# Engine order of the feed-forward products from a list of operations with durations and due times, and all low halves of the weights made on VectorE

## The chip, the cores and the metric

One core of a Trainium2 chip. A core has TensorE (PE, matrix products), VectorE (DVE), ScalarE (ACT), GpSimd (POOL) and the SP queue, each with an instruction queue of its own that runs in order and waits on semaphores; 16 DMA engines move data. The metric is the time of one execution on the device in microseconds, lower is better. "Row" below is a row of the profile or of an engine's instruction order.

## The reference

One block of a hybrid network on 256 tokens of 2048 channels, in float32: a feed-forward, a mixer (an RWKV recurrence and a pooling branch, gated), and a second feed-forward, each with a norm ahead and behind.

```python
def _swiglu(x, w_gate, w_up, w_down):          # w_gate, w_up: 2048 x 5632, w_down: 5632 x 2048
    return (jax.nn.silu(x @ w_gate) * (x @ w_up)) @ w_down

f = _swiglu(_rmsnorm(h, ln_ffn1_pre), ffn1_gate, ffn1_up, ffn1_down)
h = h + 0.5 * _rmsnorm(f, ln_ffn1_post)
mx = _hybrid_mixer(_rmsnorm(h, ln_mix_pre), w_in, ..., w_out)
h = h + _rmsnorm(mx, ln_mix_post)
f = _swiglu(_rmsnorm(h, ln_ffn2_pre), ffn2_gate, ffn2_up, ffn2_down)
h = h + 0.5 * _rmsnorm(f, ln_ffn2_post)
```

## The kernel before

**Numbers in halves.** Each weight tile `w` (128 x 1024, two rows of 128 x 512) is loaded by SP's queue, ScalarE casts it to a rounded high half `wH`, and VectorE subtracts to get the low half `wL`. A product is three matmuls of 128 x 512 (`mm3`, lines 178 to 180: high by high, high by low, low by high), once for each half `h` of the 256 tokens. Four buffers hold loaded tiles (`W32_BUFS`), five hold `wH` and `wL` (`WS_BUFS`).

**Blocks.** A feed-forward computes gate and up in 11 blocks of 512 columns. Blocks 0 and 1 are plain products. Blocks 2 to 10 (`FAST`, function `seven`) take gate (`wf`, banks f0 and f1) and up (`wl`, banks l0 and l1) together: three *quads* each replace eight products by seven through sums of the weights (`t13`, `t24`, made by VectorE in lines 407, 411 and 415; both are shown as `t`) and sums of the input (`sm`, function `sums`), into extra banks shown as `ms`; the other ten *pairs* are plain, twelve matmuls each. When the last quad is done, ScalarE copies one extra bank (line 446) and VectorE adds the others and then f0, f1, l0 and l1 (lines 449 and 465, all into tiles `u`), which empties those banks for the next block. After that come SiLU (line 750), the product of gate and up (line 754), VectorE's transposes into `T` (line 653) and 16 small transfers on GpSimd's queue (line 665, `x<-T`); ScalarE and VectorE split what arrived into halves again (`carry_at`, lines 677 and 681), the hidden rows for the down product. The down products (`post`, tables `DOWN`, `OUT`) use the same `seven` with 7 and 8 quads.

**What sets the order.** In the feed-forwards and in the last product of each stage the order on TensorE, ScalarE and VectorE is written by a recording layer: `put(t, fn)` appends matmuls with a length `t` and `at(t, fn)` gives other work a moment on that clock; `run` emits both by time. The moment of a tile's load and of both its halves is one and the same, when the slot of `WS_BUFS` comes free (`slot`). GpSimd's and SP's instructions are emitted in the same pass, and each of these two queues runs in the order of emission. The rest of the mixer is ordered by a scheduler.

**Blocks 3 to 6** (`PROBE`) treat one of their ten pairs (the up pair at row tile 12) differently, by `low_by` (line 325): it has a load of its own and halves outside the five slots, given in `seven` by `other`. ScalarE makes `dH` (line 335). The low half `dL` is made without VectorE: in the first feed-forward ScalarE writes the rounded `w` with its sign turned (line 337) and a transfer on GpSimd's queue adds `w` to it (line 341); in the second GpSimd subtracts (line 343). The three steps are emitted at fixed moments ahead of the product:

```python
        s.at(t - 24, get)
        s.at(t - 18, high)
        s.at(t - 17.9, low)
```

Of the kernel before, what the change touches and what calls it, by code (L numbers as in the profile page):

```python
# [14 lines left out]
ALU = mybir.AluOpType  # L15
# [23 lines left out]
TT = 0.45  # L39
NUNITS = 33  # L40
STAG = 10
TRAIL = 16
AHEAD = (5.0, 6.0)
TURNS = [[4.2, 5.3, 6.4, 7.5], [5.3, 6.0, 6.7, 7.4]]
WARM = 12
TB = 4
DOWN = ((0, 7, ((8, 12), (0, 3, 5, 7, 9)), 0),
        (2, 8, ((2, 4, 6, 8, 10, 12), (0, 2)), TRAIL))
OUT = ((0, 0, (), 0), (1, 2, ((4,), (0,)), 0), (3, 0, (), TRAIL))
FAST = range(2, 11)  # L50
PROBE = range(3, 7)
CARRY = (18, 21)
NG, SPOTS = 3, ((2, 4), (1,))
# [3 lines left out]
ROWS2 = [("r_k", 8), ("gn_w", 8), ("gn_b", 8), ("pool_scale", 8)]  # L57


class Block:  # L60
    def __init__(s, tc, ctx):
# [5 lines left out]
        s.late, s.after, s.items, s.events, s.now = [], [], deque(), [], 0.0  # L67
        s.clk, s.uses = 0.0, []
# [35 lines left out]
    def at(s, t, fn):  # L104

        s.n += 1
        heapq.heappush(s.events, (t, s.n, fn))

    def slot(s, end):

        s.uses.append(end)
        n = len(s.uses) - 1 - WS_BUFS
        return s.uses[n] if n >= 0 else n - 1.0

    def run(s):

        s.now = 0.0
        E = mybir.EngineType
        with s.tc.manual_schedule(engines={E.PE, E.Activation, E.DVE}):
            while s.items or s.events:  # L120
# [7 lines left out]
        s.now = s.clk = 0.0  # L128
        s.uses = []

    def put(s, t, fn):
        s.items.append((t, fn))
        s.clk += t
# [48 lines left out]
    def gemm_tok(s, w, c0, at, KT, evac, lead=False, trail=False, xs=None, hold=False,  # L182
                 order=None):
# [11 lines left out]
        def both(k0, k1):  # L195
            for k2 in order or range(k0, k1, 4):
                keep(s.load_w(w, k2, min(4, k1 - k2), c0, 512))
                for k in range(k2, min(k2 + 4, k1)):
                    do(k, 0)
                    do(k, 1)  # L200

        if trail:
            both(0, KT - TRAIL)
            s.by_half(w, c0, KT - TRAIL, KT, s.clk, AHEAD[0], do, keep,
                      lambda h: evac(h, pss[h]))
            return
        k0 = 0
        if xs:
            s.head(w, c0, KT, do, keep, xs)
            k0 = KT  # L210
        elif lead:
            s.by_half(w, c0, 0, STAG, s.clk, AHEAD[1], do, keep)
            s.run()
            k0 = STAG
        both(k0, KT)
        if hold:
            for h in range(2):
                s.at(0.3 + 1.6 * h, lambda h=h: evac(h, pss[h]))
            return
        with s.tc.high_priority(offset=BOOST):  # L220
            for h in range(2):
                evac(h, pss[h])

    def gemm_at(s, w, c0, at, KT, evac):

        pss = []
        ws = {}

        def load(k):
            ws.update((i, (wH, wL)) for i, wH, wL in s.load_w(w, k, 2, c0, 512))  # L230

        def do(k):
            if not pss:
                pss.extend(s.pm.tile([P, 512], F32, tag="mm", name=s.nm("mm"))
                           for _ in range(2))
            for h in range(2):
                (wH, wL), (xH, xL) = ws[k], at(k)
                s.mm3(pss[h], xH[:, h * P:h * P + P], xL[:, h * P:h * P + P], wH, wL,
                      k == 0, k == KT - 1)
        for k in range(0, KT, 2):  # L240
            s.at(s.slot(s.clk + 12 * MM), lambda k=k: load(k))
            s.put(6 * MM, lambda k=k: do(k))
            s.put(6 * MM, lambda k=k: do(k + 1))
        for h in range(2):
            s.at(s.clk + 0.3 + 1.6 * h, lambda h=h: evac(h, pss[h]))

    def by_half(s, w, c0, k0, k1, start, ahead, do, keep, done=None):

        for k in range(k0, k1, 2):
            s.at(start + (k - k0) * 3 * MM - ahead,  # L250
                 lambda k=k: keep(s.load_w(w, k, 2, c0, 512, k - k0 >= STAG)))
        for h in range(2):
            for k in range(k0, k1):
                s.put(3 * MM, lambda k=k, h=h: do(k, h))
            if done:
                s.put(0, lambda h=h: done(h))

    def sums(s, T, out, when, own=None, nq=2):
# [4 lines left out]
        fl = lambda t: t.rearrange("p a b t -> p (a b t)")  # L263

        def first():
            xH, xL = [t[:, :2 * nq].bitcast(F32).rearrange("p k t -> p (k t)")
                      for t in T[len(out) // 2]]
            x = tt["x"] = s.unit((P, 2, 2, S), F32, "sx")[:, :nq]
            V.tensor_tensor(out=fl(x), in0=xH, in1=xL, op=ALU.add)

        def second():
            x = tt["x"]
# [10 lines left out]
        def parts():  # L283

            j = len(out) // 2
            for n_ in ("sH", "sL"):
                if j % 2 == 0:
                    own["12" + n_] = s.unit((P, 2, 2, 2, P), F32R, n_)
                if j == 0:
                    own["4" + n_] = s.unit((P, 4, 2, P), F32R, n_)  # L290
            x = T[j]
            s3 = [u.rearrange("p (i b) t -> p i b t", b=2)[:, :, 0, P:] for u in x]
# [3 lines left out]
                       ([u[:, j] for u in s4], f[:, 3]), (s3, f[:, 2])]  # L296
# [3 lines left out]
        def lows():  # L300
# [3 lines left out]
            for i in range(2):  # L304
                out.append([(s12[0][:, m, i], s12[1][:, m, i]) for m in range(2)]
                           + [tuple(u[:, i] for u in v) for v in (s3, s4)])
# [9 lines left out]
        def fourth():  # L316
            f, fH, fL = tt["f"], tt["H"], tt["L"]
            V.tensor_tensor(out=fl(fL), in0=fl(f), in1=fl(fH).bitcast(F32), op=ALU.subtract)
            for i in range(nq):
                out.append([(fH[:, m, i], fL[:, m, i]) for m in range(4)])  # L320
        for i, fn in enumerate((first, second) + ((parts, lows) if own is not None
                                                  else (third, fourth))):
            s.at(when + 1.7 * i, fn)

    def low_by(s, how, w, k, c0, t, keep):

        nc = s.nc
        x = {}

        def get():  # L330
            x["w"] = s.get_w(w, k, 2, c0, 512, own=True)

        def high():
            x["H"], x["L"] = s.unit(dt=F32R, p="dH"), s.unit(dt=F32R, p="dL")
            nc.scalar.copy(x["H"], x["w"])
            if how == "dma":
                nc.scalar.activation(out=x["L"], in_=x["w"], func=AF.Copy, scale=-1.0)

        def low():
            if how == "dma":  # L340
                nc.gpsimd.dma_start(out=x["L"], in_=x["w"], accum_op=ALU.add)
            else:
                nc.gpsimd.tensor_tensor(out=x["L"], in0=x["w"], in1=x["H"].bitcast(F32),
                                        op=ALU.subtract)
            H, L = [x[n].rearrange("p (k c) -> p k c", k=2) for n in "HL"]
            keep([(k + i, H[:, i], L[:, i]) for i in range(2)])
        s.at(t - 24, get)
        s.at(t - 18, high)
        s.at(t - 17.9, low)

    def seven(s, wf, cf, wl, cl, at, KT, T, sm, n, spots, ev_first, ev_last, trail=0,
              one_end=False, ends=(-0.05, 2.7), other=None):
# [3 lines left out]
        V = nc.vector  # L356
        K0 = 2 * n

        bank = {}
        std = KT - K0  # L360
        left = dict(f0=std + n, f1=std, l0=std + n, l1=std + n, p1=n, p5=n, p6=n, p7=n)

        def mul(b, x, wt):
            left[b] -= 1
            new = b not in bank
            if new:
                bank[b] = s.psum("ms") if b[0] == "p" else s.pm.tile(
                    [P, 512], F32, tag="mm", name=s.nm("mm"))
            s.mm3(bank[b], *x, *wt, new, left[b] == 0)
# [4 lines left out]
        ws = {}  # L374

        def keep(tiles):
            ws.update((k, (wH, wL)) for k, wH, wL in tiles)

        def pair(k, w, c0, b):
            if other and (b, k) == other[1]:  # L380
                s.low_by(other[0], w, k, c0, s.clk, keep)
            else:
                s.at(s.slot(s.clk + 12 * MM), lambda: keep(s.load_w(w, k, 2, c0, 512)))
# [5 lines left out]
            s.put(12 * MM, do)  # L389
# [1246 lines left out]
```

## Time and profile before

| | |
|---|---|
| three executions, median (lowest to highest) | 2050.68 us (2049.8 to 2051.21) |
| profiled execution, first to last instruction (span) | 2047.8 us |
| TensorE, VectorE, ScalarE, GpSimd busy | 2019.4, 1741.7, 1161.5, 337.8 us |
| products of 128 x 512 into the plain banks (lines 178, 179, 180) | 3 x 2200 |
| TensorE's granted clock, mean | 0.997 of full speed |
| transfers | 425.66 MB, 208 GB/s |

The profiled execution is one of its own, known by its span; the executions that are timed are longer by what lies around the span, some 2.9 us at the median. Busy is the time in which an engine works on an instruction. A matmul's length is modelled and overlaps the next one's, so a busy TensorE is not TensorE at its peak. A wait is idle time of an engine, put down to the instruction that ended it. Names after "<-" are what an instruction reads; buffer numbers are left out.

### The profile page before, as it was taken

To read this page: it belongs to the slowest core of one execution; us is meant where nothing else is said; L and a number is where in the kernel's file an instruction comes from. 1 tells how busy PE (TensorE), PEld (TensorE's weight loads), DVE (VectorE), ACT (ScalarE), POOL (GpSimd) and SP (SyncE) were. 2 spreads that over 40 slices of the span, in tenths; PEclk is the share of its full clock that TensorE was granted. 3 is DMA by queue.
4 is the path that set the end of the run, shared out by engine and by line. 5 is a ranking of instruction groups with operands and counts; after the bars stand their busy time and mean duration, and the time that the engine had idled before them with its cause. 6 is when DMAs were issued, how large, how long until landed. Compare 5 with 4: busy or idle time off the path is not lost.

```text
span 2047.8 us, 28810 instructions
## 1 busy us (share of the span) xinstructions
PE 2019.4 (99%) x10011; PEld 1664.0 (81%) x10011; DVE 1741.7 (85%) x2296; ACT 1161.5 (57%) x1563; POOL 337.8 (16%) x681
## 2 busy tenths in 40 slices
PE   9999999999999999999999999999999999999997
PEld 7887778888888888878788788888877888888886
DVE  6998889999998867789689577869989999999986
ACT  7555555555555566675576444565555555555553
POOL 0122111211000023402320111001222213110000
PEclk9999999999999999999999999999999999999999
DMA  7667776666667777757556557666666666766674
GB/s 259 194 202 240 219 219 211 203 220 212 207 213 257 226 212 213 205 162 213 147 171 187 162 170 265 216 216 195 213 200 213 215 198 213 219 215 195 216 258 144
DMA packets 227418, 425.66 MB, mean 208 GB/s; under 512 B 24127, under 2 KB 27593, under 8 KB 227273
## 3 DMA queue, kind: packets, MB, share of 16 engines
q1 hardware_dynamic: 204137, 384.70, 60.4%
q0 software_dynamic: 22848, 38.61, 6.1%
q8 instruction: 79, 1.29, 0.3%
q10 hardware_dynamic: 288, 0.52, 0.1%
q14 instruction: 66, 0.54, 0.1%
HBM read 396.69 MB, written 8.39 MB: 198 GB/s over the span
## 4 chain that ended last, share of the span: by engine, by line
PE 81%; DVE 8%; issue 4%; DMA 3%; ACT 2%; POOL 0%; DVEq 0%; ACTq 0%; POOLq 0%; SPq 0%
PE mm L178 23%; PE mm L180 23%; PE mm L179 23%; PE ms L179 3%; PE ms L180 3%; PE ms L178 3%; DVE wL L155 2%; DMA w<-in_ffn_gate_dram 2%; DVE u L449 1%; DMA w<-in_ffn_up_dram 1%; ACT wH L154 1%; DVE t L407 1%; DVE wL L423 1%; ACT wH L422 1%; PE tr L635 1%
## 5 line engine op out<-in xcount | busy, mean ns | idle before, releaser
L178 PE MATMUL mm<-wH,xH 128*128 128x512 f32 x2200 | 859.4, 391 | 4.8 <-DVE u L449 3.7
L179 PE MATMUL mm<-wL,xH 128*128 128x512 f32 x2200 | 855.3, 389 | 5.0 <-DVE wL L155 5.0
L180 PE MATMUL mm<-wH,xL 128*128 128x512 f32 x2200 | 854.6, 388 | 0.7 <-DVE xL L643 0.7
L155 DVE TENSOR_TENSOR wL<-w,wH 128x1024 fp32r<-128x1024 f32 (+1 forms) x543 | 655.2, 1220 | 205.7 <-ACT wH L154 199.6
L154 ACT CAST wH<-w 128x1024 fp32r<-128x1024 f32 (+1 forms) x543 | 557.9, 1044 | 342.5 <-PE mm L180 245.1
L178 PEld LDWEIGHTS mm<-wH,xH 128*128 128x128 f32 x2200 | 413.4, 188 | 94.4 <-issue 6.8
L179 PEld LDWEIGHTS mm<-wL,xH 128*128 128x128 f32 x2200 | 413.5, 188 | 90.6 <-DVE wL L155 8.3
L180 PEld LDWEIGHTS mm<-wH,xL 128*128 128x128 f32 x2200 | 413.4, 188 | 86.2 <-DVE xL L643 1.5
L422 ACT CAST wH<-t 128x1024 fp32r<-128x1024 f32 x172 | 181.1, 1054 | 291.9 <-DVE t L415 172.0
L665 POOL DMA_DIRECT2D x<-T x352 | 173.0, 502 | 687.7 <-DVE T L653 317.2
L423 DVE TENSOR_TENSOR wL<-t,wH 128x1024 fp32r<-128x1024 f32 x172 | 209.6, 1221 | 10.9 <-ACT wH L422 6.4
L423 DVE TENSOR_TENSOR wL<-w,wH 128x1024 fp32r<-128x1024 f32 (+1 forms) x172 | 163.1, 948 | 1.1 <-ACT wH L422 1.1
L422 ACT CAST wH<-w 128x1024 fp32r<-128x1024 f32 (+1 forms) x172 | 140.6, 832 | 30.5 <-DMA w<-in_ffn_down_dram 15.3
L407 DVE TENSOR_TENSOR t<-w,w 128x1024 f32<-128x1024 f32 x86 | 104.8, 1218 | 2.5 <-DMA w<-in_ffn_down_dram 2.5
L179 PE MATMUL ms<-wL,sH 128*128 128x512 f32 x174 | 67.7, 389 | 0.0
L178 PE MATMUL ms<-wH,sH 128*128 128x512 f32 x174 | 67.7, 389 | 0.0
L180 PE MATMUL ms<-wH,sL 128*128 128x512 f32 x174 | 67.7, 389 | 0.0
L449 DVE TENSOR_TENSOR u<-ms,u 128x512 f32<-128x512 f32 x92 | 61.4, 686 | 1.4
L718 POOL DMA_DIRECT2D R<-R x96 | 47.2, 499 | 83.8 <-issue 57.6
L411 DVE TENSOR_TENSOR t<-w,t 128x512 f32<-128x512 f32 x86 | 58.9, 685 | 0.0
L415 DVE TENSOR_TENSOR t<-w,t 128x512 f32<-128x512 f32 x86 | 58.8, 684 | 0.0
L845 POOL DMA_DIRECT2D gb<-in_ln_ffn_post_dram x4 | 2.2, 558 | 284.7 <-PE mm L180 142.6
(333 smaller groups left out, 2068.2 us busy)
## 6 DMA issues: line engine op xcount, KB each, us to landing
w<-in_w_in_dram SPq DMA_DIRECT2D x128, 512.0 KB
w<-in_ffn_up_dram SPq DMA_DIRECT2D x122, 512.0 KB
w<-in_ffn_gate_dram SPq DMA_DIRECT2D x120, 512.0 KB
w<-in_ffn_down_dram SPq DMA_DIRECT2D x116, 512.0 KB
w<-in_ffn_down_dram SPq DMA_DIRECT2D x120, 256.0 KB
w<-in_ffn_gate_dram SPq DMA_DIRECT2D x112, 256.0 KB
w<-in_ffn_up_dram SPq DMA_DIRECT2D x108, 256.0 KB
w<-in_w_out_dram SPq DMA_DIRECT2D x28, 512.0 KB
```

Source lines behind the costliest of these rows:

```text
L154: s.nc.scalar.copy(vH, v)
L155: s.nc.vector.tensor_tensor(out=vL, in0=v, in1=vH.bitcast(F32), op=ALU.subtract)
L178: nc.tensor.matmul(ps, aH, bH, start=start, stop=False)
L179: nc.tensor.matmul(ps, aH, bL, start=False, stop=False)
L180: nc.tensor.matmul(ps, aL, bH, start=False, stop=stop)
L407: V.tensor_tensor(out=v["t13"], in0=v["a"], in1=v["b0"].to_broadcast([P, 2, 512]), op=ALU.subtract)
L411: V.tensor_tensor(out=v["t24"][:, 0], in0=v["a"][:, 0], in1=v["t13"][:, 1], op=ALU.add)
L415: V.tensor_tensor(out=v["t24"][:, 1], in0=v["b"][:, 0], in1=v["t24"][:, 0], op=ALU.subtract)
L422: nc.scalar.copy(H, v[n_])
L423: V.tensor_tensor(out=L, in0=v[n_], in1=H.bitcast(F32), op=ALU.subtract)
L449: V.tensor_tensor(out=u[o], in0=bank[b], in1=u[i], op=ALU.add)
L665: nc.gpsimd.dma_start(out=x[0][q * 32:q * 32 + 32, i], in_=src[i * 32:i * 32 + 32, q])
```

## The change

The clock with fixed moments is replaced by a list. Each operation becomes a `Node` with its engine, an assumed duration, a lag until others see its result, a due time worked out from TensorE's clock, and the nodes that it needs. `asks` and `give` hand out the buffers of `CAPS`. `play` walks through the list in assumed time: TensorE takes its products in the given order, and ScalarE, VectorE, GpSimd and the loads each take, among what is ready, the operation with the earliest due time; as each is taken, its instruction is emitted. `low_by` and `PROBE` are gone, so that all ten pairs of blocks 3 to 6 are ordinary (`feed`). The sums for `FAST` read the normalised rows directly instead of joining two halves. The order of quads and pairs, written now as strings, is the one before ("q" a quad, "f" and "l" a gate or up pair). The up product of block 0 and the spreading of the norm's factors come into the list too.

```diff
-DOWN = ((0, 7, ((8, 12), (0, 3, 5, 7, 9)), 0),
-        (2, 8, ((2, 4, 6, 8, 10, 12), (0, 2)), TRAIL))
-FAST = range(2, 11)
-PROBE = range(3, 7)
-CARRY = (18, 21)
-NG, SPOTS = 3, ((2, 4), (1,))
+LAG = dict(P=0.2, A=0.18, V=0.16, G=0.2, D=2.4, N=0.0)
+CAPS = dict(w=W32_BUFS, ws=WS_BUFS, u=1)
+FAST = {b: "fffqffqllqlll" for b in range(2, 11)}
+DOWN = ((0, "fffffffffqffffqfflqlllqllqllqllqlllll", 0),
+        (2, "fffqffqffqffqffqffqflqllqlll", TRAIL))
+va = lambda m: 0.07 + m / 960
+aa = lambda m: 0.09 + m / 1200
...
-    def run(s):
-        s.now = 0.0
...
-                while s.events and (s.events[0][0] <= s.now or not s.items):
-                    heapq.heappop(s.events)[2]()
-                if s.items:
-                    t, fn = s.items.popleft()
-                    fn()
-                    s.now += t
+    def play(s, order, wait):
...
+            t, e = best
+            if e == "P":
+                n = order.popleft()
+            else:
+                while soon[e] and soon[e][0][0] <= t:
+                    n = heapq.heappop(soon[e])[2]
+                    heapq.heappush(now[e], (n.due, n.n, n))
+                n = heapq.heappop(now[e])[2]
+            n.left = -1
+            free[e] = t + n.dur
+            n.fn()
+            done(n, t + n.dur + n.lag)
...
+    def feed(s, w, k, n, c0, t, hold=False):
...
+        g = s.job("D", 1.75 * m / 1024, get, t - 9, take="w")
+        h = s.job("A", aa(m), high, t - va(m) - aa(m) - 0.5, (g,), None if hold else "ws")
+        return b, s.job("V", va(m), low, t - va(m) - 0.3, (h,), give=("w",))
...
-    def low_by(s, how, w, k, c0, t, keep):
...
         def pair(k, w, c0, b):
-            if other and (b, k) == other[1]:
-                s.low_by(other[0], w, k, c0, s.clk, keep)
-            else:
-                s.at(s.slot(s.clk + 12 * MM), lambda: keep(s.load_w(w, k, 2, c0, 512)))
+            ws, l = s.feed(w, k, 2, c0, s.clk)
...
-            s.at(m + 0.2, start)
-            for j, a in enumerate(((1, "p6", 0), (2, "p7", 1), (1, "p5", 1), (3, "p5", 2))):
-                s.at(m + 0.7 + gap * j, lambda a=a: add(*a))
+            j0 = s.job("A", 0.5, start, t, (e,), "u")
+            j1 = plus(1, "p6", 0, t, j0)
+            j2 = plus(2, "p7", 1, t + 0.6, j1)
+            j3 = plus(1, "p5", 1, t + 1.2, j2)
+            j4 = plus(3, "p5", 2, t + 1.8, j2)
...
-        s.at(t, move)
-        for h in range(2):
-            s.at(t + CARRY[h], lambda h=h: high(h))
-            s.at(t + CARRY[h] + 2, lambda h=h: low(h))
+        ms = [s.job("G", 0.49, lambda i=i, q=q: move(i, q), t, turned, lag=4.0) for i, q in iq]
+        hs = [s.job("A", aa(512), lambda h=h: high(h), t + 10, ms) for h in range(2)]
+        return s.job("N", 0, None, 0, [s.job("V", va(512), lambda h=h: low(h), t + 11, (hs[h],))
+                                       for h in range(2)])
```

Three places show how the instructions move. First, ScalarE's queue in block 6 of the first feed-forward, from the second quad's casts to the third quad's first, before and after (`w` a loaded tile, `t` a sum of weights, `xH<-x` the carried rows):

```order
L422 CAST wH_2703<-w_1314_2694 128x1024
L422 CAST wH_2716<-w_1315_2695 128x512
L422 CAST wH_2731<-t_1316_2700 128x1024
L422 CAST wH_2747<-t_1317_2701 128x1024
L335 CAST dH_2763<-w_1326_2729 128x1024
L337 ACTIVATE dL_2764<-w_1326_2729 128x1024
L154 CAST wH_2770<-w_1333_2768 128x1024
L154 CAST wH_2782<-w_1336_2780 128x1024
L422 CAST wH_2798<-w_1339_2789 128x1024
```

```order
L530 CAST wH_2699<-w_2665_2652 128x1024
L530 CAST wH_2734<-w_2668_2664 128x512
L530 CAST wH_2737<-t_2682_2716 128x1024
L809 CAST xH_2759<-x_2664_2633 128x4x128
L530 CAST wH_2762<-t_2683_2717 128x1024
L809 CAST xH_2759<-x_2664_2633 128x4x128
L281 CAST wH_2777<-w_2679_2703 128x1024
L281 CAST wH_2785<-w_2684_2719 128x1024
L530 CAST wH_2794<-w_2689_2742 128x1024
```

The `dH` cast and the activation behind it are gone from ahead of the two pairs' casts, and the carried rows' casts have moved up from behind the third quad to the second quad's end.

Second, VectorE's queue at the end of the same block, from the last quad's last low half (before: the row behind it) to the adds that empty the banks, before and after (`ms` the quads' extra banks, `mm` the plain banks):

```order
L681 TENSOR_TENSOR xL_2853<-x_1305_2654,xH_2852 128x4x128
L155 TENSOR_TENSOR wL_2859<-w_1353_2856,wH_2858 128x1024
L155 TENSOR_TENSOR wL_2872<-w_1356_2869,wH_2871 128x1024
L155 TENSOR_TENSOR wL_2881<-w_1359_2878,wH_2880 128x1024
L681 TENSOR_TENSOR xL_2853<-x_1305_2654,xH_2852 128x4x128
L155 TENSOR_TENSOR wL_2894<-w_1362_2891,wH_2893 128x1024
L155 TENSOR_TENSOR wL_2906<-w_1365_2903,wH_2905 128x1024
L449 TENSOR_TENSOR u_2922<-ms_2721,u_2921 128x512
L449 TENSOR_TENSOR u_2923<-ms_2712,u_2922 128x512
L449 TENSOR_TENSOR u_2922<-ms_2708,u_2922 128x512
L449 TENSOR_TENSOR u_2924<-ms_2708,u_2923 128x512
L449 TENSOR_TENSOR u_2922<-mm_2608,u_2922 128x512
```

```order
L534 TENSOR_TENSOR wL_2848<-t_2702_2798,wH_2847 128x1024
L287 TENSOR_TENSOR wL_2861<-w_2703_2800,wH_2860 128x1024
L287 TENSOR_TENSOR wL_2868<-w_2708_2828,wH_2867 128x1024
L287 TENSOR_TENSOR wL_2877<-w_2709_2832,wH_2876 128x1024
L287 TENSOR_TENSOR wL_2889<-w_2712_2851,wH_2888 128x1024
L570 TENSOR_TENSOR u_2908<-ms_2707,u_2907 128x512
L570 TENSOR_TENSOR u_2909<-ms_2695,u_2908 128x512
L570 TENSOR_TENSOR u_2908<-ms_2691,u_2908 128x512
L570 TENSOR_TENSOR u_2910<-ms_2691,u_2909 128x512
L570 TENSOR_TENSOR u_2908<-mm_2593,u_2908 128x512
L287 TENSOR_TENSOR wL_2917<-w_2719_2879,wH_2916 128x1024
L570 TENSOR_TENSOR u_2910<-mm_2597,u_2910 128x512
```

One pair's low half and both carried halves no longer stand ahead of the adds; a pair's low half stands between the last two adds of gate banks.

Third, VectorE's queue in the block that follows, around the carried rows' lows. Before, they stand behind the third quad (the first five rows of the fence above are that place one block earlier). After, in the second quad, 14 rows behind the block's two transposes:

```order
L287 TENSOR_TENSOR wL_3063<-w_2738_2966,wH_3062 128x1024
L513 TENSOR_TENSOR t_2764_3091<-w_2747_3027,w_2750_3039 128x1024
L534 TENSOR_TENSOR wL_3075<-w_2747_3027,wH_3074 128x1024
L517 TENSOR_TENSOR t_2765_3092<-w_2747_3027,t_2764_3091 128x512
L534 TENSOR_TENSOR wL_3110<-w_2750_3039,wH_3109 128x512
L521 TENSOR_TENSOR t_2765_3092<-w_2750_3039,t_2765_3092 128x512
L534 TENSOR_TENSOR wL_3113<-t_2764_3091,wH_3112 128x1024
L813 TENSOR_TENSOR xL_3135<-x_2746_3008,xH_3134 128x4x128
L534 TENSOR_TENSOR wL_3138<-t_2765_3092,wH_3137 128x1024
L813 TENSOR_TENSOR xL_3135<-x_2746_3008,xH_3134 128x4x128
```

The carried rows' lows have moved up by eight and eleven rows, over the whole third quad, to either side of the second quad's last low half.

More of the change, by code (lines that the diff above doesn't have):

```diff
@@ L66, in __init__ @@
         s.nxt = None
-        s.late, s.after, s.items, s.events, s.now = [], [], deque(), [], 0.0
-        s.clk, s.uses = 0.0, []
+        s.late, s.after = [], []
+        s.clk, s.order, s.asks, s.freed, s.jobs = 0.0, [], {}, {}, []
         s.cp = E(tc.tile_pool(name="cp", bufs=1))
@@ L363, in mul @@
         def mul(b, x, wt):
             left[b] -= 1
[L365 to L369, printed above, removed]
+            new = b not in pss
+            s.mm3(s.bank(pss, b), *x, *wt, new, left[b] == 0)
         def rows(k, h):
```

901 lines of the change are left out of this document (544 added, 357 removed).

## The prediction

> **What bounds the kernel now.** I read the page's busy shares first, then who TensorE waited for, then stretches of the trace, then single instructions at one wait.
>
> ```profile
> span 2047.8 us, 28810 instructions
> PE 2019.4 (99%) x10011; PEld 1664.0 (81%) x10011; DVE 1741.7 (85%) x2296; ACT 1161.5 (57%) x1563; POOL 337.8 (16%) x681
> ```
>
> TensorE is the bound: it is busy for all but 28.4 us. VectorE is next. The change leaves the same matmuls in almost the same order, so all that it can win lies in what TensorE waits for. The view of waits, for TensorE alone, in the two stretches that hold the feed-forwards' gate and up products (130 to 450 us, 1480 to 1660 us):
>
> ```profile
> PE mm L178 <- DVE u L449: 2.0, 5, 0.6
> PE mm L179 <- DVE wL L155: 1.6, 3, 0.8
> PE mm L178 <- ACT wH L154: 0.5, 1, 0.5
> ...
> PE mm L179 <- DVE wL L155: 3.4, 3, 1.9
> PE mm L178 <- DVE u L449: 1.6, 3, 0.9
> ```
>
> (Columns: total, times, longest.) That is 4.1 us in nine waits and 5.0 us in six, 9.1 us in 15. Busy time and granted clock by stretch, block by block (blocks 3, 4, then 6, 7, 8 of the first feed-forward, some 42 us each):
>
> ```profile
> 140.00:182.00 42.00, 41.31 (x183) 33.88 (x182) 37.63 (x43) 24.93 (x29) 8.76 (x17) 1.00 0.73 225
> 183.00:225.00 42.00, 41.65 (x184) 34.13 (x183) 37.86 (x44) 24.23 (x28) 8.81 (x17) 1.00 0.72 222
> ...
> 269.00:311.00 42.00, 40.72 (x179) 33.15 (x177) 36.42 (x42) 23.82 (x28) 8.81 (x17) 1.00 0.69 210
> 312.00:354.00 42.00, 41.65 (x185) 34.28 (x183) 39.95 (x47) 23.60 (x28) 7.87 (x16) 1.00 0.66 210
> 354.00:396.00 42.00, 42.00 (x187) 34.80 (x186) 40.18 (x46) 24.10 (x29) 7.84 (x16) 1.00 0.69 213
> ```
>
> (PE, PEld, DVE, ACT, POOL busy, clock, DMA.) This is the row that decides. Blocks 3 to 6 carry a low half made off VectorE, and TensorE loses time in them although VectorE works least there (36.4 to 37.9 of 42 us). Blocks 7 and 8 make every low on VectorE, which is then 95% busy (40.18 of 42), and TensorE has no gap but the one at 312 that block 6 left behind. So VectorE's load is not what makes TensorE wait. The timeline of block 6 shows what does (ACT, DVE, PE):
>
> ```profile
> 289.63 1.05 ACT L335 CAST dH<-w 128x1024 fp32r<-128x1024 f32 x1 [2.87 <-DMA w<-in_ffn_up_dram]
> 290.58 1.05 ACT L337 ACTIVATE dL<-w 128x1024 fp32r<-128x1024 f32 x1
> 291.54 1.98 ACT L154 CAST wH<-w 128x1024 fp32r<-128x1024 f32 x2
> ...
> 292.60 2.36 DVE L155 TENSOR_TENSOR wL<-w,wH 128x1024 fp32r<-128x1024 f32 x2 [4.59 <-ACT wH L154]
> ...
> 292.62 0.50 PE L178 MATMUL mm<-wH,xH 128*128 128x512 f32 x1 [0.52 <-ACT wH L154]
> 293.88 0.50 PE L179 MATMUL mm<-wL,xH 128*128 128x512 f32 x1 [0.76 <-DVE wL L155]
> ```
>
> ScalarE's queue stood 2.87 us at `dH`, whose load had not landed; two casts that TensorE needs earlier stood behind it; VectorE idled 4.59 us for them. Then the lost time comes back a second time, 20 us later:
>
> ```profile
> 306.94 1.05 ACT L154 CAST wH<-w 128x1024 fp32r<-128x1024 f32 x1 [1.89 <-PE mm L180]
> 307.90 0.57 ACT L446 COPY u<-ms 128x512 f32<-128x512 f32 x1
> ...
> 309.17 2.73 DVE L449 TENSOR_TENSOR u<-ms,u 128x512 f32<-128x512 f32 x4
> 311.81 1.28 DVE L449 TENSOR_TENSOR u<-mm,u 128x512 f32<-128x512 f32 x2
> ```
>
> The copy that opens the block's merge stands behind a cast that waits for TensorE, the adds come late, and the next block's first matmul waits for the bank that they empty.
>
> **What 15 waits cost.** A wait costs more than its idle time, because a matmul's shown length reaches beyond the next one's start:
>
> ```profile
> 182.66 0.39 PE L179 MATMUL mm<-wL,xH 128*128 128x512 f32 x1
> 182.88 0.39 PE L180 MATMUL mm<-wH,xL 128*128 128x512 f32 x1
> 183.62 0.47 PE L178 MATMUL mm<-wH,xH 128*128 128x512 f32 x1 [0.35 <-DVE u L449]
> ...
> 1578.16 0.50 PE L179 MATMUL mm<-wL,xH 128*128 128x512 f32 x1 [1.94 <-DVE wL L155]
> 1581.89 0.63 PE L180 MATMUL mm<-wH,xL 128*128 128x512 f32 x1
> ...
> 1580.00:1584.00 4.00, 4.00 (x13) 3.13 (x13) 4.00 (x6) 1.62 (x2) 0.00 (x0) 0.69 0.81 265
> ```
>
> Starts are 0.22 to 0.23 us apart; here 0.74 for an idle of 0.35, so 0.16 more: 15 x 0.16 = 2.4 us. After the longest wait the granted clock falls to 0.69, and the ten spacings from 1578.16 to 1581.89 take 3.73 us instead of 10 x 0.227 = 2.27: 1.5 us. In all 9.1 + 2.4 + 1.5 = 13.0 us.
>
> **The change, part by part.**
>
> *The eight lows go back to VectorE.* Removed: eight `dH` casts and four `dL` activations on ScalarE in their places, four accumulating transfers, four GpSimd subtractions. Added: eight casts and eight subtractions in the ordinary five-slot stream. The load of that pair now stands six places later on SP's queue, in line with the pairs around it, and the casts behind it no longer wait for it. Price on VectorE, from starts:
>
> ```profile
> 326.50 1.22 DVE L423 TENSOR_TENSOR wL<-w,wH 128x1024 fp32r<-128x1024 f32 x1
> 327.63 0.69 DVE L411 TENSOR_TENSOR t<-w,t 128x512 f32<-128x512 f32 x1
> 328.24 0.69 DVE L423 TENSOR_TENSOR wL<-w,wH 128x512 fp32r<-128x512 f32 x1
> ...
> 1574.64 2.39 POOL L343 TENSOR_TENSOR dL<-w,dH 128x1024 fp32r<-128x1024 f32 x1 [6.91 <-ACT dH L335]
> 1575.54 3.70 DVE L155 TENSOR_TENSOR wL<-w,wH 128x1024 fp32r<-128x1024 f32 x2 [3.60 <-ACT wH L154]
> ...
> L269 DVE TENSOR_TENSOR sx<-xH,xL 128x1024 f32<-128x1024 f32 (+1 forms) x13 | 14.8, 1137 | 0.0
> ```
>
> 1.13 us for a full tile, 0.60 for a half: 8 x 1.13 = 9.0 us more. Against it, two subtractions that ran beside GpSimd's took 3.70 us where two without it take 2.36 (at 292.60): 1.34 us, four times, 5.4 us given back. And four of the 13 joins go (two full, two half): 3.5 us. Net about +0.1 us on VectorE over the whole kernel, +1.1 us in each of blocks 3 to 6 of the first feed-forward. The cover is VectorE's spare of blocks 7 and 8: 1.8 us of 42. If that were gone, each us would be TensorE's.
>
> The Trainium skill (Perfetto Trace Analysis, section Optimizing Scalar/DVE Operations) says that with a saturated VectorE it can pay to move work to ScalarE or even GpSimd, but that GpSimd and VectorE share an SBUF read port, so that moving between these two may not help. The first half speaks against this change; by it the eight lows would be a loss, which is the second rival below. With the second half the trace agrees: 3.70 against 2.36 us.
>
> *The merge comes sooner.* Behind the last quad's last low VectorE had five lows and two carried halves ahead of the adds (5 x 1.13 + 2 x 0.60 = 6.9 us); now four lows (4.5 us), and ScalarE's copy stands behind four casts instead of five. 2.3 us more room against u-waits of at most 0.9 us. This is the cover against the added 1.1 us.
>
> *The carried halves move up.* `xH<-x` on ScalarE and `xL<-x` on VectorE now come 14 VectorE instructions behind the transposes, eight of 1.13 and six of 0.60: 12.6 us. What they wait for:
>
> ```profile
> 320.12 7.87 POOL L665 DMA_DIRECT2D x<-T  x16 [27.26 <-DVE T L653]
> ...
> x<-T POOLq DMA_DIRECT2D x352, 32.0 KB, 3.5
> h<-hsp POOLq DMA_DIRECT2D x8, 512.0 KB, 6.7
> ...
> L677 ACT CAST xH<-x 128x512 fp32r<-128x512 f32 x44 | 27.0, 614 | 0.0
> ```
>
> 7.9 us of issue, 3.5 to land, 0.6 of cast: 12.0 us. It fits with 0.6 us to spare where before it never waited (idle 0.0). ScalarE will stand at `xH`, with the next quad's cast behind it. Cost between 0 and, at a landing like the 6.7 us of the 512 KB reloads, 3.2 - 0.6 - 1.8 = 0.8 us a block; I take 0, since the same transfer of the same size measured 3.5.
>
> *The rest.* The order of quads and pairs, the last half-by-half products and the tail after the last matmul are the same instructions; the last block and the down products had no TensorE wait from 440 to 700 us (260 of 260 busy), with VectorE at 235.06 of 260. SP's and GpSimd's queues keep their order but for the eight loads and the eight lows. Bounds: 0.9 us gained (the one transpose wait, 0.7 + 0.16) to 1.6 us lost at the two places where block 0's up product and the normalised rows now come from the list (twice 0.8, the longest wait on `wL` in the first feed-forward); taken as 0. The middle block is left to the scheduler as before, with a few rows swapped: +-0.5, taken as 0.
>
> ```profile
> 440.00:700.00 260.00, 260.00 (x1149) 215.24 (x1148) 235.06 (x272) 146.41 (x172) 19.34 (x39) 1.00 0.70 223
> PE tr L635 <- DVE fg L877: 0.7, 1, 0.7
> ```
>
> **Sum.** 13.0 us of waits; the one at 437 us (0.40 + 0.16) comes from a block without a probe, so I count 12.4. The executions' median is 2050.68, 2.9 us above the profiled span of 2047.8; that remainder is unchanged. 2050.7 - 12.4 = 2038.3, and 2035.4 as a span.
>
> **Rivals.**
> *Only the first kind of wait goes.* The eight waits on `u` stay, 3.6 + 8 x 0.16 = 4.9 us: 2050.7 - 13.0 + 4.9 = 2042.6. For it: 95% of VectorE; against it: the 2.3 us and block 8, which has none.
> *VectorE becomes the bound.* All 9.0 us of lows reach TensorE: 2050.7 - 13.0 + 9.0 = 2046.7, a change that can hardly be measured. For it: 40.18 of 42 us; against it: no gap in block 8 at that very load. This is what the first half of the Trainium skill's sentence (Perfetto Trace Analysis, above) would give.
> *Slower: the carried cast blocks ScalarE.* 22 carries (352 / 16). Once a landing passes 3.5 + 0.6 + 1.8 = 5.9 us, what is over comes 22 times; at 6.5 us the 13 us are used up, at 6.7 us the kernel stands at 2050.7 - 13.0 + 22 x 0.8 = 2055.3. For it: the cast's new place, and the transfers now run right under the weight loads; against it: the measured 3.5.
>
> **How the numbers follow.** First case 0.64, its own range 2036 (all 13.0 us and the transpose's 0.9 gone: 2036.8, less a little) to 2041 (2.7 us of new short waits); only the first kind 0.16; VectorE the bound 0.11; the carried cast 0.09. 0.2% is 4.1 us, about what a measurement of this kernel tells from no change. Below 2046.6 lie the first two and 0.04 of the third: 0.84. Between 2046.6 and 2054.8 lie 0.07 of the third and 0.03 of the carried cast, where it is mild: 0.10. Above: 0.06. The range goes from 2034.5, the first case's end with the 1.6 us of the two starts and the 0.5 of the middle counted the other way, to 2045, past the first rival; it leaves out 0.20.
>
> **What would show it.** Right: no wait on `wL` between 130 and 450 us or 1480 and 1660 us, TensorE 42 of 42 us in blocks 3 to 6 with VectorE near 40; u-waits under 1 us in all; a clock of 1.00 there. Wrong: waits on `u` in as many blocks as before (first rival), VectorE at 42 of 42 with `wL` waits (second), ScalarE's idle time before `xH` of over 2 us a block with `wH` late behind it (third). What would make the whole wrong is a wait in the down products, where I see no reason for one.

## The result

Four executions of the kernel after have a median of 2032.62 us (2032.0 to 2033.49), four of the kernel before beside them 2050.94: ratio 0.9915, 95% interval 0.9901 to 0.9929, 18.3 us faster. The forecast of 2038.3 had the sign and the place of most of the gain, but the time lies 1.9 us below its range.

The page of the kernel after:

```profile
span 2031.8 us, 28759 instructions
PE 2014.8 (99%) x10011; PEld 1664.1 (82%) x10011; DVE 1735.4 (85%) x2300; ACT 1164.7 (57%) x1559; POOL 326.6 (16%) x673
```

TensorE's waits (total, times, longest), the whole list of 0.2 us or more but for the start's:

```profile
PE ms L265 <- DVE wL L534: 1.4, 2, 0.8
PE ms L264 <- ACT wH L530: 1.0, 1, 1.0
PE pS L1691 <- ACT R L1685: 0.7, 1, 0.7
PE mm L266 <- DVE xL L777: 0.5, 1, 0.5
```

The 15 waits of the feed-forwards' gate and up products are gone. New are three into `ms`. Busy time by stretch, block 3, then the block with the first new wait:

```profile
140.00:182.00 42.00, 42.00 (x187) 34.76 (x187) 40.02 (x46) 24.07 (x28) 7.86 (x16) 1.00 0.69 218
...
394.00:430.00 36.00, 35.24 (x155) 28.53 (x154) 31.69 (x35) 20.59 (x24) 7.85 (x16) 1.00 0.70 218
```

TensorE 42.00 of 42 with VectorE at 40, as forecast. The new waits come in one block of each feed-forward: one wait in block 9 of the first (TensorE at 412 us) and two in block 7 of the second (1646 us). Here is the second place (ScalarE, GpSimd's queue, TensorE):

```profile
1636.04 1.05 ACT L530 CAST wH<-t 128x1024 fp32r<-128x1024 f32 x1
1643.95 0.62 ACT L809 CAST xH<-x 128x512 fp32r<-128x512 f32 x1 [6.86 <-DMA x<-T]
1644.48 1.04 ACT L530 CAST wH<-t 128x1024 fp32r<-128x1024 f32 x1
...
1627.65 0.50 POOL L797 DMA_DIRECT2D x<-T  x1 [32.74 <-issue]
1631.02 3.92 POOL L797 DMA_DIRECT2D x<-T  x8 [2.87 <-issue]
...
1645.57 0.50 PE L264 MATMUL ms<-wH,sH 128*128 128x512 f32 x1 [0.96 <-ACT wH L530]
```

ScalarE stands 6.86 us at the carried cast, since GpSimd's small transfers came late: from the first issue to the last landing these 16 took 16.2 us, the other 21 groups of 16 took 10.3 to 13.7. The quad's `wH` behind the cast is then late for TensorE. It is the mechanism of the third rival, in one block of nine. In the first feed-forward's block 9 ScalarE stands 5.57 us at the same cast.

**Where the 16.0 us between the two profiled spans lie.** The kernels can be laid side by side from one instruction to another that all of them have. The marks, here with their times in a kernel without waits (the old one with `PROBE` empty, second experiment):

```profile
129.80 0.39 PE L178 MATMUL ms<-wH,sHL 128*128 128x512 f32 x1
...
686.72 0.39 PE L178 MATMUL mm<-kH,xH 128*128 128x512 f32 x1
...
862.01 0.39 PE L1274 MATMUL pn<-bones,R 128*128 128x2 f32 x3
...
910.34 0.50 PE L178 MATMUL mm<-wH,yb 128*128 128x512 f32 x1
```

From the first product by `sHL` (block 2) to the first by a held tile `kH` (last of the down products) I call a feed-forward's body; from `pn` to the first product by `yb` the mixer's state part. Differences of such starts in us, and TensorE's idle times of over 0.15 us added up:

| profile | body 1 | state part | body 2 | TensorE idle in the bodies |
|---|---|---|---|---|
| before | 563.81 | 51.97 | 565.30 | 9.2 |
| before, second profile | 566.09 | 51.97 | 567.64 | 12.2 |
| after | 558.27 | 48.33 | 559.61 | 2.4 |
| after, second profile | 557.08 | 48.31 | 557.31 | 0 |
| before, no low off VectorE | 556.92 | 48.33 | 556.92 | 0 |
| before, loads earlier | 556.96 | 51.97 | 557.03 | 0 |
| before, casts later | 560.67 | 51.97 | 563.23 | 6.3 |
| before, second feed-forward's alone | 556.92 | 48.33 | 568.21 | 8.4 |
| after, lows put back in the list | 557.07 | 51.95 | 559.44 | 0.9 |
| after, carry lag 9.0 | 556.92 | 48.34 | 556.92 | 0 |
| after, carry lag 8.0 | 556.92 | 51.94 | 556.92 | 0 |
| after, carry lag 0.5 | 575.94 | 48.33 | 576.82 | 17.1 |

Before to after: bodies 5.5 and 5.7, state part 3.6, the transposes ahead of the mixer 0.5 (their wait of 0.67 on `fg`), the start 0.4 and the tail behind the last matmul 0.6, less 0.4 at the second feed-forward's start: 15.9, the 16.0 but for rounding. The medians differ by 2.3 us more. The profiled execution after took 2033.49 us, 0.9 above its median; the other 1.4 lie with the first execution before, whose own time is not known; that it was a short one is likely (the second profile has 3 us more of idle time) but not shown.

A body in which TensorE has no such wait takes 556.92 to 557.31 us, whatever the order of the other engines. What lies above that comes with waits.

### The profile page after: what moved, and what is told of

It reads as the page before. It is cut to its first block, busy times and chain, and to the rows that moved or that the text cites. A ratio compares the mean times of both kernels' runs of the same rounds, so it can differ in the third digit from the quotient of the medians.

```text
span 2031.8 us, 28759 instructions
## 1 busy us (share of the span) xinstructions
PE 2014.8 (99%) x10011; PEld 1664.1 (82%) x10011; DVE 1735.4 (85%) x2300; ACT 1164.7 (57%) x1559; POOL 326.6 (16%) x673
## 4 chain that ended last, share of the span: by engine, by line
PE 97%; issue 1%; DMA 1%; DVE 1%; ACT 1%; POOL 0%; DVEq 0%; POOLq 0%; SPq 0%; ACTq 0%
PE mm L264 27%; PE mm L266 27%; PE mm L265 27%; PE ms L266 4%; PE ms L265 4%; PE ms L264 4%; PE tr L768 1%; DMA x<-T 0%; PE pA L1575 0%; PE mc L728 0%; PE pU L1671 0%; DMA w<-in_ffn_gate_dram 0%; PE pSa L1683 0%; PE pY L1706 0%; PE pT L1742 0%
## 5 line engine op out<-in xcount | busy, mean ns | idle before, releaser
L264 PE MATMUL mm<-wH,xH 128*128 128x512 f32 (+1 forms) x2232 | 871.6, 391 | 0.0
L266 PE MATMUL mm<-wH,xL 128*128 128x512 f32 (+1 forms) x2232 | 866.5, 388 | 0.6 <-DVE xL L777 0.5
L265 PE MATMUL mm<-wL,xH 128*128 128x512 f32 (+1 forms) x2232 | 866.6, 388 | 0.2
L281 ACT CAST wH<-w 128x1024 fp32r<-128x1024 f32 x373 | 388.1, 1053 | 231.3 <-PE mm L266 139.5
L287 DVE TENSOR_TENSOR wL<-w,wH 128x1024 fp32r<-128x1024 f32 x373 | 449.4, 1221 | 77.8 <-ACT wH L281 72.0
L241 DVE TENSOR_TENSOR wL<-w,wH 128x1024 fp32r<-128x1024 f32 (+3 forms) x178 | 209.9, 1188 | 82.7 <-ACT wH L240 81.2
L240 ACT CAST wH<-w 128x1024 fp32r<-128x1024 f32 (+3 forms) x178 | 182.1, 1027 | 149.7 <-PE mm L266 129.3
L530 ACT CAST wH<-w 128x1024 fp32r<-128x1024 f32 (+1 forms) x172 | 143.1, 834 | 70.7 <-PE mm L266 32.5
L534 DVE TENSOR_TENSOR wL<-w,wH 128x1024 fp32r<-128x1024 f32 (+1 forms) x172 | 163.7, 952 | 5.2 <-ACT wH L530 5.0
L513 DVE TENSOR_TENSOR t<-w,w 128x1024 f32<-128x1024 f32 x86 | 105.0, 1220 | 12.2 <-DMA w<-in_ffn_down_dram 7.6
L570 DVE TENSOR_TENSOR u<-mm,u 128x512 f32<-128x512 f32 x92 | 61.1, 683 | 11.0 <-PE mm L266 11.0
```

The source lines that it names most:

```text
L240: s.nc.scalar.copy(vH, v)
L241: s.nc.vector.tensor_tensor(out=vL, in0=v, in1=vH.bitcast(F32), op=ALU.subtract)
L264: nc.tensor.matmul(ps, aH, bH, start=start, stop=False)
L265: nc.tensor.matmul(ps, aH, bL, start=False, stop=False)
L266: nc.tensor.matmul(ps, aL, bH, start=False, stop=stop)
L281: s.nc.scalar.copy(b["H"][:, :m], b["w"][:, :m])
```

## The experiments

The kernels ran on three chips: the first, second, third and fifth below on one, the later casts and the carry lag of 0.5 on another, the rest on a third. Each ratio is to executions of the kernel before on the same chip.

### The kernel before once more

> The kernel before, unchanged, for a second profile beside the first, to see what one execution's span is worth. If the profiled executions scatter like the timed ones, the span lies between 2046.5 and 2050 us and the remainder between the span and the execution's own time is 1.5 to 2 us, as in the kernel after (2033.49 against 2031.8); then some 2 us of the 18.3 us between the medians are only the first profile's short execution. If the remainder of 2.9 us of the prediction is real, it shows again here, and the kernel after has lost 1.2 us of it.

2055.88 us with a span of 2054.1; the seven executions beside it have a median of 2054.07 (2052.45 to 2055.53). The same waits, longer:

```profile
PE mm L179 <- DVE wL L155: 8.5, 8, 2.1
PE mm L178 <- ACT wH L154: 2.1, 3, 1.3
```

10.6 us in eleven waits, and 1.6 in five on `u`. The remainder here is 1.8 us; elsewhere it was 1.7 to 3.4, so it is no constant to add to a span. What differs between the two profiles is how late the separate loads land: from issue to landing the eight took 5.6 to 7.6 us in the first and 6.3 to 8.4 in the second. ScalarE's `dH`, first and second profile (the last number is its idle time there):

```profile
L335 ACT CAST dH<-w 128x1024 fp32r<-128x1024 f32 x8 | 8.4, 1051 | 13.9 <-DMA w<-in_ffn_up_dram 13.9
...
L335 ACT CAST dH<-w 128x1024 fp32r<-128x1024 f32 x8 | 8.4, 1051 | 21.0 <-DMA w<-in_ffn_up_dram 21.0
```

### No low half off VectorE, old order

```diff
-PROBE = range(3, 7)
+PROBE = ()
```

> The kernel before with PROBE empty: the old order of fixed moments, and all low halves on VectorE. Theory 1 (the eight lows made off VectorE are the loss): all 15 waits of the gate and up stretches go, 13.0 us, and the mixer's stretch from 868 to 921 us gets VectorE's new order and with it the 3.65 us that the kernel after won there: 2050.9 - 13.0 - 3.65 = 2034.3, between 2033 and 2036. Theory 2 (the list's order is the gain): with 9.0 us more of lows in the old order VectorE is late, waits on wL and u of 5 us or more stay, 2041 to 2047. No wait of the carried halves (xH idle 0.0) under either, since these stand where they stood.

2030.27 us (2029.7 to 2034.53), ratio 0.9889 (0.9873 to 0.9906): 23.8 us less than the kernel before on its chip. No wait in either body is left; of 0.6 us or more the whole list is:

```profile
PE warm L514 <- POOL ident masks.py:199: 1.7, 1, 1.7
PE pS L1473 <- ACT R L1467: 0.7, 1, 0.7
PE tr L635 <- DVE fg L877: 0.7, 1, 0.7
...
130.00:690.00 560.00, 560.00 (x2472) 463.69 (x2471) 522.49 (x597) 317.95 (x367) 73.88 (x150) 1.00 0.67 219
```

Theory 1 stands: one line of the old kernel gives the whole gain. VectorE at 522.49 of 560 (512.94 before) does not make TensorE wait. The list is not what wins. The time expected was 4 us too long, because it took the waits of the first profile, and these at the prediction's 13.0 us; on this chip they cost more, 9.2 us in body 1 and 10.7 in body 2 by the second profile, with 3.6 for the state part: 23.5 of the 23.8.

### The lows kept, their loads earlier; or their casts later

```diff
-        s.at(t - 24, get)
+        s.at(t - 34, get)
```

> The kernel before with the eight separate loads issued 34 instead of 24 us ahead of their product, nothing else. If the waits come from dH standing at the head of ScalarE's queue for a load that has not landed, dH's idle time on ScalarE falls to near 0 and most of the 15 waits go: 2038 to 2042 (the mixer is as before). If they come from the lows themselves (the transfers, GpSimd beside VectorE, the one act more on ScalarE), the waits stay: 2047 to 2052. In the second feed-forward the longest wait, 1.94 us on wL at 1578 us, which stands beside a 3.70 us pair of VectorE, should then stay.

2035.84 us, ratio 0.9911 (0.9896 to 0.9925), less than the 2038 to 2042 expected, as all waits of both bodies went. SP's queue shows what was late. Before, around block 6, then with the earlier load:

```profile
280.41 2.95 SPq L140 DMA_DIRECT2D w<-in_ffn_up_dram  x3
...
270.26 0.43 SPq L140 DMA_DIRECT2D w<-in_ffn_up_dram  x1
...
284.28 1.05 ACT L335 CAST dH<-w 128x1024 fp32r<-128x1024 f32 x1
```

Of the three issues at 280.41 the separate load is the third. Ahead of it in the queue stand the loads of the two pairs that follow, and these wait for VectorE to free a tile; on ScalarE those two pairs' casts stand *behind* `dH`. So the load that is needed first is issued last. Issued at 270.26 it is there at 284.28 without idle time (`dH`: 0.0 for all eight, 13.9 before). The low halves made off VectorE cost TensorE nothing here:

```profile
1563.37 2.50 POOL L343 TENSOR_TENSOR dL<-w,dH 128x1024 fp32r<-128x1024 f32 x1 [3.99 <-ACT dH L335]
...
1564.31 3.77 DVE L155 TENSOR_TENSOR wL<-w,wH 128x1024 fp32r<-128x1024 f32 x2 [0.71 <-ACT wH L154]
...
1455.00:1660.00 205.00, 205.00 (x905) 169.54 (x904) 196.13 (x219) 116.91 (x135) 49.22 (x84) 1.00 0.67 215
```

VectorE's pair still takes 3.77 us beside GpSimd's subtraction, and TensorE is busy for 205.00 of 205 us. The Trainium skill (SBUF — State Buffer, section Who interferes with whom) says that a VectorE instruction with two SBUF inputs contends with a GpSimd instruction that reads SBUF; the trace agrees, 3.77 against 2.36 us, but this was not what TensorE waited for. The Trainium skill (Perfetto Trace Analysis, section Optimization Strategy) reads a gap that repeats as a possible lack of SBUF or PSUM for the next tile; here the earlier loads left the number of buffers as it was, and the gap went with the order of a queue.

```diff
-        s.at(t - 18, high)
-        s.at(t - 17.9, low)
+        s.at(t - 11, high)
+        s.at(t - 10.9, low)
```

> The kernel before with the separate casts dH and the lows behind them emitted 11 instead of 18 us ahead of the product, the loads as before. The other way to keep dH from standing ahead of a load that has not landed. Theory: dH's idle on ScalarE (13.9 us, 21.0 in the second profile) falls to near 0, the waits of blocks 3 to 6 go, feed-forwards' blocks 557 us each, the mixer as before: 2035 to 2037, like the kernel with the earlier loads. The low halves still come in time (two casts and 5 us of transfer make 7 of the 11 us). Rival (early loads help through something else, such as the transfers' times): waits stay, over 2045.

2042.74 us, ratio 0.9945 (0.993 to 0.996). Half right: `dH` idles 0.0 us and the waits on `wL` are gone from the pairs, but the merge is late instead:

```profile
PE mm L178 <- DVE u L449: 5.9, 7, 1.5
...
221.12 0.58 ACT L446 COPY u<-ms 128x512 f32<-128x512 f32 x1
```

`dH` and the activation now stand just ahead of the block's last casts, and the copy that opens the merge starts at 221.12, where it starts at 217.81 in the kernel without them (which leads by only 0.5 us at that point). My expectation looked only at the wait taken away.

### The lows put back as operations of the list

```diff
...
+        g = s.job("D", 1.75, get, t - 24, rel=t - 24)
+        h = s.job("A", aa(1024) * (2 if how == "dma" else 1), high, t - 18, (g,))
+        return b, s.job("G", 0.93 if how == "dma" else 2.4, low, t - 17.9, (h,),
+                        lag=5.0 if how == "dma" else 0.2)
...
```

> The kernel after with the eight off-VectorE lows put back as operations of the list (load due 24 us ahead of the product, cast 18 us ahead but ordered behind its load's assumed landing). Theory 1 (whatever the order, these lows cost): waits in blocks 3 to 6 of both feed-forwards come back, at least half of the 12.4 us: 2039 or more, and VectorE's pairs beside GpSimd's subtraction take 3.7 us again. Theory 2 (the order was at fault, since the list puts no cast at the head of ScalarE's queue before its load is due): no wait above 0.5 us in blocks 3 to 6, and apart from the mixer's stretch, which gets another VectorE order here (up to 3.65 us), the time stays within 1.5 us of the kernel after: 2031 to 2037.

2037.24 us, ratio 0.9918 (0.9903 to 0.9933). `dH` idles 0.0: the list, which puts a cast behind the assumed landing of its load, takes that wait away as well. In body 1, with all four transfers that add, there is no wait (557.07). Theory 2 is right that far: there, leaving the lows out and ordering them well are two ways to the same 557 us. Less the state part's 3.6 us the span of 2034.6 us comes to 2031.0, between the kernel after's two profiles (2031.8 and 2028.7).

In body 2, with the four subtractions on GpSimd, two waits on `wL` of 0.9 us in all are left, and the body takes 2.5 us more than one without waits. Ahead of the first wait, at 1567.65, VectorE works for 12 us without idle time; one of its subtractions, beside GpSimd's, takes 3.83 us in place of 1.22. Ahead of the second, at 1609.93, two beside GpSimd's take 4.55 us in place of 2.50, and ScalarE then stands 3.63 us at `xH`. So a low that GpSimd makes is not free in every order.

### Half of the lows

`PROBE` as before for the second feed-forward alone.

> The kernel before with the off-VectorE lows in the second feed-forward alone; VectorE's order in the mixer is that of the kernel after. If the parts add: first feed-forward's blocks 577.3 us as without any (before: 584.2 and 586.5 in its two profiles), mixer 868 to 921 us 48.3 (before: 52.0), second feed-forward's blocks 565 to 568 as before with its waits on wL of 1 to 2 us. The time lies 8.3 to 10.7 us above the kernel without any (ratio 0.9889): ratio 0.993 to 0.994. If GpSimd's subtractions do no harm by themselves, dH's idle time on ScalarE in the second feed-forward (about 8 us of the 13.9) is there beside each wait.

2042.47 us, ratio 0.9941 (0.9929 to 0.9954); the kernel with none, on another chip, had 0.9889. The parts add: 556.92, 48.33 and 568.21. `dH` idles 11.6 us in four places, where I expected 8, and beside them stand four waits on `wL` of 1.65 to 2.10 us, 7.7 in all, at and above the upper end of what I expected.

### The kernel after once more, and the carried casts

> The kernel after, unchanged, on the chip of the runs beside it, for a comparison by stage on one chip. Theory: the new waits in block 9 of both feed-forwards (0.67, 0.96 and 0.76 us, with what follows them 1.3 and 2.6 us) belong to the kernel and not to one execution, and come again within 1 us. Rival: they are scatter of the transfers and are gone or elsewhere. Time against the kernel before 0.989 to 0.993, since the kernel before varies by some 2 us from one set of runs to the next and this one does not.

2031.24 us (2030.41 to 2038.6), ratio 0.9896 (0.9881 to 0.991). My theory was wrong: no wait of 0.2 us or more is left in the bodies (557.08 and 557.31, against 558.27 and 559.61). The expectation also has the place of the second feed-forward's waits wrong, block 9 for block 7. But ScalarE stands at `xH` nearly as long, after and second profile:

```profile
L809 ACT CAST xH<-x 128x512 fp32r<-128x512 f32 x44 | 26.8, 617 | 62.4 <-DMA x<-T 59.5 <-DVE wL L534 2.9
...
L809 ACT CAST xH<-x 128x512 fp32r<-128x512 f32 x44 | 26.8, 618 | 53.3 <-DMA x<-T 53.3
```

So the kernel seems to be at an edge, where it depends on how late the transfers of an execution are whether TensorE waits; two profiles alone do not show that. Three kernels move the casts, by the assumed lag of the carried transfers:

```diff
-        ms = [s.job("G", 0.49, lambda i=i, q=q: move(i, q), t, turned, lag=4.0) for i, q in iq]
+        ms = [s.job("G", 0.49, lambda i=i, q=q: move(i, q), t, turned, lag=9.0) for i, q in iq]
```

> The kernel after with one number changed: the carried transfers' assumed lag is 9.0 us instead of 4.0, so that the casts xH<-x stand three or four weight casts later in ScalarE's queue. VectorE's order in the mixer is that of the kernel after. Theory (the carried casts at the head of ScalarE's queue, waiting for transfers, make the new waits): xH's idle time on ScalarE falls from 62.4 us to under 20, both waits of block 9 are gone, first feed-forward's blocks 577.3 us (after: 578.7), second's 557.0 (after: 559.6), 4.0 us in all: 2028.6. Rival (the waits come from VectorE at 95% or from the loads): they stay, within 1 us of the kernel after.

2030.19 us, ratio 0.9884 (0.9871 to 0.9898). `xH` never idles (0.0), and both bodies take 556.92 us. Against the kernel after that is 4.0 us by its first profile and 0.5 by its second; the intervals of the two ratios overlap.

> The kernel after with the carried transfers' assumed lag at 0.5 us instead of 4.0: in each block the first cast xH<-x stands three rows further up in ScalarE's queue, the second two. VectorE's order in the mixer is that of the kernel after. It gives the price of a carried cast that stands too early. At 26 ScalarE rows to 42 us a row is 1.6 us, so xH waits some 3 to 5 us longer in each of the 22 carries: idle 53 to 62 us becomes 120 to 170. Theory (ScalarE's room ahead of TensorE is used up at about 5 us: an idle of 4.33 us before xH cost nothing, 5.57 us cost 1.3): TensorE then waits for wH and wL of the quads in most of the 18 blocks, 1 to 2.5 us each: 2045 to 2075, slower than or near the kernel before. Rival (the waits of block 9 were scatter of other things): TensorE does not wait, 2030 to 2034, whatever xH's idle.

2072.89 us, ratio 1.0098 (1.0081 to 1.0115), slower than the kernel before:

```profile
L809 ACT CAST xH<-x 128x512 fp32r<-128x512 f32 x44 | 26.8, 618 | 129.8 <-DMA x<-T 129.8
...
PE ms L265 <- DVE wL L534: 10.5, 17, 0.8
PE mm L264 <- ACT wH L530: 4.5, 4, 1.9
```

Besides these there are seven of 2.8 us on `mm`; 17.1 us of all this lie in the bodies. Two or three rows up ScalarE's queue cost 38.9 us in the bodies, and the time is within the range expected. An idle time of 53 us at `xH` cost 0.5 us; of the 77 us more, half comes through. The reading that fits is that ScalarE runs a few us ahead of TensorE, and that it is late once that lead is used up, here in nearly every block; the lead itself was not measured. This is the mechanism of the third rival, brought about by an earlier place of the cast and not by later landings, and it is large enough to undo the whole gain.

> As with a lag of 9.0, but 8.0: for the feed-forwards nearly the same order, while the scheduler that orders the mixer now falls into VectorE's old order there. It separates the mixer's part by itself. Theory (the 3.65 us between 868 and 921 us are only VectorE's order there): the feed-forwards as with 9.0 to 0.5 us, the waits on R and sgb of the mixer (1.3, 1.1 and 0.6 us) are back, and the time is 3.6 us longer than with 9.0: 2032.2. Rival (the gain in the mixer comes from the new order of the feed-forward, for instance of GpSimd's or SP's queue): no difference between 8.0 and 9.0 there.

2033.59 us, ratio 0.9899 (0.9884 to 0.9914), 3.4 us above the lag of 9.0. The bodies are equal to 0.01 us; the state part is 51.94 against 48.34, and the waits there are those of the kernel before:

```profile
PE pA L1575 <- DVE R L1551: 1.3, 2, 1.1
...
PE pB L1594 <- DVE R L1586: 1.1, 2, 0.8
...
PE mm L264 <- ACT sgb L1210: 0.6, 1, 0.6
```

VectorE's and ScalarE's instructions of the state part stand with a lag of 8.0 in the very order of the kernel before. With 9.0, as in the kernel after, both orders differ in several places, on VectorE from 8 us behind `pn` on. Here is the place beside the longest wait, VectorE before and after, from the last `L1335` (`L1553`) products on:

```profile
901.31 2.82 DVE L1335 TENSOR_TENSOR R<-R,R 64x512 f32<-64x512 f32 x4
904.16 1.23 DVE L155 TENSOR_TENSOR wL<-w,wH 128x1024 fp32r<-128x1024 f32 x1
...
905.70 1.39 DVE L1333 TENSOR_TENSOR R<-R,R 64x512 f32<-64x512 f32 x2
...
892.41 2.82 DVE L1553 TENSOR_TENSOR R<-R,R 64x512 f32<-64x512 f32 x4
895.26 0.68 DVE L1551 TENSOR_TENSOR R<-R,R 64x512 f32<-64x512 f32 x1
...
896.26 1.21 DVE L241 TENSOR_TENSOR wL<-w,wH 128x1024 fp32r<-128x1024 f32 x1
```

A weight's low half that stood ahead of the first `R` product, for which TensorE's `pA` waits, now stands behind it. How the 3.6 us divide among the rows that moved was not tested. The mixer's code is the same; its scheduler falls into the one order or the other with a number as far away as a lag of the feed-forward. All twelve profiles have 51.94 to 51.97 or 48.31 to 48.34.

## Why the prediction was right and where it failed

*What bounds the kernel: right.* TensorE's waits, not VectorE's load, and `dH` at the head of ScalarE's queue as their source: with the load earlier and nothing else, all of them go.

*What 15 waits cost: too low.* 13.0 us forecast; 563.81 + 565.30 less twice 556.92 is 15.3. A wait on a fresh tile's first product shows 0.76 us of idle time but puts the next start 1.03 late, and the start behind it 0.10 more; I had read 0.16 from one wait of another kind. Time lost to idle time was 1.7 to 1 here (15.3 to 9.2), 1.6 in the second profile (19.9 to 12.2), 2.3 with the carried casts three rows up (38.9 to 17.1), 1.3 with a few long waits (second feed-forward's lows alone, 11.3 to 8.4).

*The lows on VectorE, free: right.* 42.00 of 42 with VectorE at 40. The second rival is excluded, and with it what the prediction drew for this kernel from the first half of the Trainium skill's sentence on a saturated VectorE: off VectorE (loads earlier) the bodies take 556.96 and 557.03 us, on it 556.92.

*The merge sooner: right.* No wait on `u` in either profile after. The first rival is excluded.

*The carried halves, taken as 0: wrong in its working.* I counted the room of 12.6 us in VectorE's rows. ScalarE reaches `xH` earlier than that, and idles there 53 to 62 us. The transfers were under-reckoned too: 7.9 + 3.5 us takes the median landing of a single one, while the cast waits for the last of 16, and from first issue to last landing the profile before shows 11.0 to 14.9 us. That all this cost only 0.5 to 4.0 us, and not what the third rival reckoned from its idle time, fits a lead of ScalarE over TensorE, which the prediction did not count.

*The rest, taken as 0: the step that failed.* "The middle block is left to the scheduler as before, with a few rows swapped: +-0.5". Those few rows were worth 3.64 us, in a place where the profile before shows five waits of 3.0 us in all (`pA`, `pB`, `sgb`), one of them 1.09 us on a row that moved; I looked at the waits of the two feed-forwards alone. With the transposes, the starts and the tail the rest came to 4.7 us. The sum by the measured terms, 15.3 - 4.0 + 4.7 = 16.0, is the distance between the spans; the forecast was 12.4. Without the 3.64 us the time would have been 2036.3, inside the range.

*The remainder outside the span, taken as unchanged: not borne out.* The prediction kept the 2.9 us between span and median; of the result's executions the median before lies 3.1 us above the profiled span, the median after only 0.8. That is why the medians are 2.3 us further apart than the spans, and 16.0 us alone would have given 2034.7, just inside the range. Part of it is likely a short first execution before, as said above; that is not shown.

## What to carry to other kernels

When an engine in the middle waits, look which queue issued its data: a load that is written early but queued behind loads that wait for buffers arrives late, and moving it is worth as much as taking its work away. Before calling rows "a few swapped", lay them beside the waits of that very stretch; where a scheduler decides, compare kernels by stage, since its side effects can be as large as the effect looked for. Price a cast that stands ahead of others by how far its engine runs ahead of the bound engine: up to that it is free, beyond it the loss came in nearly every block here.

## What the hardware showed that I had not expected

Two idle times of the same length can differ in what follows. Second profile before, two waits:

```profile
1496.30 0.50 PE L179 MATMUL mm<-wL,xH 128*128 128x512 f32 x1 [2.09 <-DVE wL L155]
1496.63 0.40 PE L180 MATMUL mm<-wH,xL 128*128 128x512 f32 x1
...
1540.85 0.50 PE L179 MATMUL mm<-wL,xH 128*128 128x512 f32 x1 [2.11 <-DVE wL L155]
...
1542.38 0.63 PE L179 MATMUL mm<-wL,xH 128*128 128x512 f32 x1
1542.81 0.63 PE L180 MATMUL mm<-wH,xL 128*128 128x512 f32 x1
...
1542.00:1546.00 4.00, 4.00 (x13) 3.10 (x12) 4.00 (x6) 1.05 (x1) 0.00 (x0) 0.57 0.78 256
```

After 2.09 us no spacing is above 0.33; after 2.11 us the granted clock falls 1.5 us later, and seven spacings are 0.42 or 0.43 and one 0.39. The 1.94 us of the prediction's wait were followed by such spacings too, while the 2.10 and 2.04 us in the run with the second feed-forward's lows alone were not: the granted clock stays 1.00 behind them. What decides between them is not shown. The Trainium skill (TensorE: Matmul & The Clock Gate, Part 1: The HAM clock gate) has an idle window of about 3.4 us before the clock halves; the 0.43 us agree with its cold rate, but the idle time seen ahead of it was less here, 1.94 and 2.11 us.
